# The transpose of the attention's probabilities, in one piece or in two halves of the keys

## The chip, the cores and the metric

The kernel runs on one core of a Trainium2 chip. The metric is the device time of one execution in microseconds (us); less is better. The times of the kernel before are 2897.93, 2901.62 and 2910.8 us, median 2901.62.

## What is computed

One encoder layer over 2048 tokens of width 1024. Cut to what matters here:

```python
h = rmsnorm(x)
c_q, c_kv, k_rope, dq, dk, dv = split(h @ w_in)
# head group A: 4 heads of latent attention, softmax over 2048 keys per query
s = einsum('bqhd,bkhd->bhqk', q_m, k_m) * scale
o_mla = einsum('bhqk,bkhd->bqhd', softmax(s), v_mla)
# head group B: 4 heads of differential attention, two softmax maps and a relative-position bias
s = einsum('bqhmd,bkhmd->bmhqk', dq, dk) * scale + bias
p = softmax(s);  a = p[:, 0] - lam * p[:, 1]
o_diff = rmsnorm(einsum('bhqk,bkhd->bqhd', a, dv)) * (1 - lam_init)
x = x + concat(o_mla, o_diff) @ w_out
x = x + square(relu(rmsnorm(x) @ w_up)) @ w_down
```

Everything is float32 at the inputs and outputs.

## The kernel before, in words

To keep float32's accuracy with 16-bit matmuls, most operands are split into a high and a low float16 part, and a product is made as high by high, high by low and low by high, summed in PSUM.

The program has four stages in order of time: the input projections (up to some 456 us), the attention (456 to about 1480 us), the output projection and the MLP's two products (a Strassen-like scheme of seven block products). The change touches the attention alone.

The attention runs over 4 heads and, in each, 16 blocks of 128 queries: 64 steps. A step makes, for one head and one query block, one softmax map of the MLA group (`soft[0]`, called d = 0) and two of the differential group (`soft[1]` and `soft[2]`, together d = 1). The work of a step, per map:

- **S** (line 735, TensorE): scores of 128 queries with 512 keys in one PSUM bank. Four chunks a map; five matmuls a chunk for MLA, two for the others: 36 in a step. There are seven PSUM banks for scores (tag D), so a chunk waits for an earlier one to be read.
- **M** (lines 745 and 750, VectorE): the maximum of each chunk, with the bias band added where it lies; **N** (755, 756): the shift of the exponential.
- **E** (line 762, ScalarE): the exponential into a float32 tile of 1024 keys (tag P; two a map, the halves hf = 0 and 1), with the row sum.
- **diff** (line 805, VectorE): for d = 1, the second map times a factor added to the first, a half at a time.
- **hi** (lines 812 and 140): the high float16 part of a half of the keys, by ScalarE for d = 1 and by GpSimd for d = 0; **lo** (line 819, GpSimd): the low part of a half, as the difference. Both go into the tile `hl[d]` (tag L).
- **T** (line 823): one DMA transpose for each d, issued by the queue of SyncE (SP): all 2048 keys, high and low part, 128 x 4096 float16, out of `hl[d]` into `pT[d]` (another L tile). There are seven L tiles.
- **pv** (lines 833 to 835, TensorE): the product with the values, in four parts of four key blocks (parts 0 and 1 use keys of the first half, 2 and 3 of the second), 12 matmuls a part, 96 in a step for both d. They add up in the one PSUM bank of tag O.
- **store** (839, ScalarE): the output scaled into an N2 tile (six of them), and a DMA to DRAM.

The order on each engine is written out by hand in the string `PROG`, run once a step: a token is an operation with its map and part. No mark means the current step, `'` the step before and `"` the one before that: T0' is the MLA transpose of the step before. `ordered` chains the instructions of each compute engine in this order. DMAs of this stage are not chained; they stand on SP's queue in the order that the planner gave them, and `set_fence` and `behind` keep certain loads (queries, keys, values, weights of the output projection) behind the last transpose issued before them. SP works off its queue in order: an issue that waits holds all behind it.

In PROG the operations of one step's d = 0 run: S, M, E in their own step, then `hi00 lo00 ... hi01 ... lo01` at its end, then in the next step `T0'` after S03 and `pv0'0` to `pv0'3`. Those of d = 1: `hi10'`, `hi11'` in the next step, `lo10" lo11" T1"` and `pv1"0` to `pv1"3` in the one after. So TensorE's order in a step is S00 to S03, S10 to S12, pv0'0, pv0'1, S13, pv0'2, S20, pv0'3, S21, S22, pv1"0, pv1"1, pv1"2, S23, pv1"3. GpSimd's is lo10", lo11", hi00, lo00, hi01, lo01.

Around the steps, `loads` fetches keys and values of the next head, one piece in a step, `load0` and `load1` fetch queries every fourth step, and in the last head `wo_step` prepares the weights of the output projection on VectorE and ScalarE. After the last step the program runs twice more with the first places empty, between parts of the output projection.

Of the kernel before, what the change touches and what calls it, by code (L numbers as in the profile page):

```python
# [13 lines left out]
F16 = mybir.dt.float16  # L14
BF16 = mybir.dt.bfloat16
AF = mybir.ActivationFunctionType
ALU = mybir.AluOpType
AX = mybir.AxisListType.X

P = 128  # L20
S = 2048
D = 1024
NT = S // P
# [27 lines left out]
def encoder_layer(ctx: ExitStack, tc: tile.TileContext, a, out, stop=None):  # L51
    nc = tc.nc
# [7 lines left out]
    def nm(s):  # L60
        uid[0] += 1
        return f"{s}_{uid[0]}"
# [3 lines left out]
    def sb(tag, shape, dt=F32):  # L66
        return work.tile(shape, dt, tag=tag, name=nm(tag), bufs=BUFS[tag])
# [16 lines left out]
    def pso():  # L84
        return psum.tile([P, 512], F32, tag="O", name=nm("O"), bufs=OB)
# [7 lines left out]
    def ordered(ins):  # L93

        e = ins.ins.engine
        if e in last:
            tc.add_manual_dep(ins.ins, last[e].name, NOSYNC, reason="order")
        last[e] = ins.ins
# [10 lines left out]
    def set_fence(*ins):  # L109
        for i in ins:  # L110
            fence[i.ins.engine] = i.ins
# [11 lines left out]
    G = nc.gpsimd  # L123
# [15 lines left out]
    def gscale(o, i, sc):  # L139
        return G.tensor_scalar(o, i, sc, 0.0, ALU.mult, ALU.add)  # L140
# [624 lines left out]
    class Step:  # L765
# [40 lines left out]

        def hi(self, d, hf):
            if hf == 0:
                self.hl[d] = sb("L", [P, 2, S], F16)
            o = self.hl[d][:, 0, 1024 * hf : 1024 * hf + 1024]  # L810
            if d:
                ordered(act(o, self.soft[d].p[hf], AF.Copy))  # L812
            else:
                ordered(gscale(o, self.soft[d].p[hf], 1.0))

        def lo(self, d, hf):
            c = slice(1024 * hf, 1024 * hf + 1024)
            hl = self.hl[d]
            ordered(G.tensor_tensor(hl[:, 1, c], self.soft[d].p[hf], hl[:, 0, c], ALU.subtract))  # L819

        def transpose(self, d):
            self.pT[d] = sb("L", [P, 2 * NT, P], F16)
            set_fence(nc.sync.dma_start_transpose(self.pT[d], self.hl[d].rearrange("p i k -> p (i k)")))

        def pv(self, d, part, parts):
            if part == 0:
                self.o[d] = pso()
            od = self.o[d][:, 0:P]
            n = NT // parts
            for kb in range(part * n, part * n + n):  # L830
                v = self.sl[d]["v"][kb // 8][:, kb % 8]
                hT_, lT_ = self.pT[d][:, kb, :], self.pT[d][:, NT + kb, :]
                ordered(mm(od, hT_, v[:, 0], start=kb == 0, stop=False))  # L833
                ordered(mm(od, hT_, v[:, 1], start=False, stop=False))  # L834
                ordered(mm(od, lT_, v[:, 0], start=False, stop=kb == NT - 1))  # L835
# [4 lines left out]
            dma(oD[self.qt][:, 4 * d + self.h, :], ob)  # L840

    PROG = """
    S00 M00 S01 S02 S03 load1 M01 T0' S10 M02 S11 lo10" M03 N0 E00 S12 pv0'0 E01 sums1' M10
    lo11" diff0' pv0'1 S13 pv0'2 S20 E02 M11 M12 E03 M13 pv0'3 N1 T1" S21 diff1' S22 M20 load0
    hi00 hi10' pv1"0 pv1"1 lo00 store0' hi01 M21 pv1"2 E10 E11 S23 E12 pv1"3 M22 M23 E13 N2 hi11' E20
    E21 lo01 E22 E23 rows1' sums0 store1"
    """

# [761 lines left out]
```

## Time and profile before

| | us |
|---|---|
| median of the three runs | 2901.62 |
| the profiled execution, its own time | 2907.15 |
| its span in the profile | 2905.4 |
| mean granted TensorE clock | 0.984 |
| attention, 45 full steps | 507.0 to 1190.0 |
| attention, 15 further steps in the last head | 1190.0 to 1421.35 |

The profile is of one execution. "Idle before" is time in which an engine had nothing to run before the instruction named, and behind the arrow stands what ended that time. Weight loads have an engine of their own in the profile (PEld) and run beside the matmuls (PE). DMA issues stand under SPq with the time that SP's sequencer spent on them; the landing is later.

### The profile page before, as it was taken

What the parts mean: (1) busy time and instruction counts of PE and PEld (TensorE: products, weight loads), DVE (VectorE), ACT (ScalarE), POOL (GpSimd) and SP (SyncE); (2) the same over time, 40 slices, a digit from 0 to 9 for tenths busy, and PEclk for the clock granted to TensorE, in tenths of its full rate; (3) what the DMA queues carried; (4) which work ended last, traced back from release to release, by engine and by line L of the source; (5) the groups of instructions that cost most, each with busy time, mean ns of one, the idle gap of its engine ahead of it and who ended that gap; (6) DMA issues with size and microseconds to landing.
All of it is one profiled execution on the core that took longest, in us unless ns stands there. A gap on an engine that the chain in (4) does not pass through costs nothing. (4 is left out here: it accounts for less than half of the span.)

```text
span 2905.4 us, 47553 instructions
## 1 busy us (share of the span) xinstructions
PE 2694.7 (93%) x16904; PEld 1576.4 (54%) x16904; DVE 2138.1 (74%) x4292; ACT 1742.2 (60%) x3814; POOL 1724.4 (59%) x1404
## 2 busy tenths in 40 slices
PE   7999998988899898889899989999999899999999
PEld 6878885655555565555555434444444344444444
DVE  8767778898888988899968777666666555555543
ACT  6544556887778888777847666666666433333332
POOL 5334435887778888778725366444444656555644
PEclk9999999999999999999999999999999999999999
DMA  5445566988888998889854654333334643333324
GB/s 191 121 118 128 138 143 166 200 196 180 182 190 185 198 193 195 196 192 195 204 178 145 227 157 145 131 131 130 130 123 162 235 160 124 113 130 131 131 94 175
DMA packets 990415, 469.31 MB, mean 162 GB/s; under 512 B 772032, under 2 KB 938944, under 8 KB 990176
## 3 DMA queue, kind: packets, MB, share of 16 engines
q1 hardware_dynamic: 990176, 466.27, 59.9%
q8 instruction: 132, 2.16, 0.3%
q14 instruction: 107, 0.88, 0.1%
HBM read 168.39 MB, written 132.12 MB: 103 GB/s over the span
## 5 line engine op out<-in xcount | busy, mean ns | idle before, releaser
L762 ACT ACTIVATE P<-D,nm,one 128x512 f32<-128x512 f32 x768 | 586.7, 775 | 149.4 <-DVE s L793 88.0
L735 PE MATMUL D<-W,X 128*128 128x512 f16 x2304 | 562.6, 383 | 23.6 <-ACT P L762 21.7
L819 POOL TENSOR_TENSOR L<-P,L 128x1024 f16<-128x1024 f32 x256 | 561.4, 2202 | 17.3 <-ACT L L812 6.5
L750 DVE TENSOR_REDUCE nmx<-D 128x1 f32<-128x512 f32 (+3 forms) x768 | 455.5, 621 | 65.6 <-PE D L735 59.1
L833 PE MATMUL O<-W,L 128*128 128x128 f16 x2048 | 368.5, 222 | 84.7 <-DMA L<-L 76.3
L1448 POOL TENSOR_TENSOR W<-W,N 128x512 f32<-128x512 f32 x192 | 242.7, 1274 | 227.9 <-DVE W L1446 222.7
L835 PE MATMUL O<-W,L 128*128 128x128 f16 x2048 | 368.1, 222 | 0.0
L834 PE MATMUL O<-W,L 128*128 128x128 f16 x2048 | 367.9, 222 | 0.0
L1446 DVE SCALAR_TENSOR_TENSOR W<-D,dsc,W 128x512 f32<-128x512 f32 x224 | 166.4, 747 | 263.1 <-PE D L136 263.1
L134 PE MATMUL D<-W,W 128*128 128x512 f16 (+2 forms) x822 | 314.2, 382 | 33.4 <-DVE P L1310 20.1
L735 PEld LDWEIGHTS <-X 128*128 128x128 f16 x2304 | 214.2, 99 | 231.8 <-issue 37.7
L140 POOL TENSOR_SCALAR L<-P 128x1024 f16<-128x1024 f32 x128 | 219.2, 1712 | 179.7 <-ACT P L762 179.7
L135 PE MATMUL D<-W,W 128*128 128x512 f16 (+2 forms) x822 | 313.6, 382 | 3.2 <-DVE W L130 3.2
L136 PE MATMUL D<-W,W 128*128 128x512 f16 (+2 forms) x822 | 313.4, 381 | 0.1
L833 PEld LDWEIGHTS <-L 128*128 128x128 f16 x2048 | 203.2, 99 | 151.7 <-DMA L<-L 123.4
L134 PE MATMUL D<-L,W 128*128 128x512 f16 (+1 forms) x644 | 249.5, 387 | 17.7 <-ACT X L1297 12.7
L134 PE MATMUL D<-L,P 128*128 128x512 f16 x648 | 247.8, 382 | 15.0 <-ACT N L1442 14.7
L135 PE MATMUL D<-L,P 128*128 128x512 f16 x648 | 247.5, 382 | 0.0
L136 PE MATMUL D<-L,P 128*128 128x512 f16 x648 | 247.5, 382 | 0.0
L136 PE MATMUL D<-L,W 128*128 128x512 f16 (+1 forms) x644 | 247.2, 384 | 0.0
L135 PE MATMUL D<-L,W 128*128 128x512 f16 (+1 forms) x644 | 247.1, 384 | 0.0
L834 PEld LDWEIGHTS <-L 128*128 128x128 f16 x2048 | 203.5, 99 | 31.0 <-issue 5.5
(421 smaller groups left out, 5731.5 us busy)
## 6 DMA issues: line engine op xcount, KB each, us to landing
P<-uD SPq DMA_DIRECT2D x124, 448.0 KB, 4.8
uD<-P SPq DMA_DIRECT2D x96, 512.0 KB, 3.2
P<-in_w_up_dram SPq DMA_DIRECT2D x34, 512.0 KB, 4.0
W<-in_w_down_dram SPq DMA_DIRECT2D x32, 512.0 KB, 4.4
X<-in_x_dram SPq DMA_DIRECT2D x17, 512.0 KB, 3.7
vD<-N SPq DMA_DIRECT2D x32, 256.0 KB, 2.6
qA<-N SPq DMA_DIRECT2D x32, 256.0 KB, 2.6
oD<-N SPq DMA_DIRECT2D x128, 64.0 KB, 2.4
```

Of the source, the lines that this page charges most:

```text
L134: mm(o, ah, bh, start=first, stop=False, skip_group_check=more),
L135: mm(o, ah, bl, start=False, stop=False, skip_group_check=more),
L136: mm(o, al, bh, start=False, stop=last, skip_group_check=more),
L140: return G.tensor_scalar(o, i, sc, 0.0, ALU.mult, ALU.add)
L735: ordered(mm(s, st, mv[:, kc], start=j == 0, stop=j == len(self.passes) - 1))
L750: ordered(V.tensor_reduce(self.nmx[:, self.n : self.n + 1], s[:, c0 * P : c1 * P], AX, ALU.max))
L762: last_exp[:] = [act(o, self.ch[c], AF.Exp, bias=self.nm, scale=self.sg, accum_out=self.sm[:, c : c + 1])]
L819: ordered(G.tensor_tensor(hl[:, 1, c], self.soft[d].p[hf], hl[:, 0, c], ALU.subtract))
L833: ordered(mm(od, hT_, v[:, 0], start=kb == 0, stop=False))
L834: ordered(mm(od, hT_, v[:, 1], start=False, stop=False))
L835: ordered(mm(od, lT_, v[:, 0], start=False, stop=kb == NT - 1))
L1448: G.tensor_tensor(x, x, part.pop((t, to)), ALU.add)
```

## The change

The transpose of each d becomes two, one for each half of the keys. The split tile `hl` is laid out with the half as the outermost index, so that the high and low part of a half lie together, and `pT` likewise. In `PROG` the second half's MLA transpose T01' takes the place of T0'; the first half's, T00, stands a step earlier, right behind lo00. Of the differential ones, T10" stands behind lo10" and T11" behind lo11"; T1" behind N1 goes. The products read their slices from the new places; they keep their places in the order.

```diff
         def hi(self, d, hf):
             if hf == 0:
-                self.hl[d] = sb("L", [P, 2, S], F16)
-            o = self.hl[d][:, 0, 1024 * hf : 1024 * hf + 1024]
+                self.hl[d] = sb("L", [P, 2, 2, 1024], F16)
+            o = self.hl[d][:, hf, 0]
...
         def lo(self, d, hf):
-            c = slice(1024 * hf, 1024 * hf + 1024)
-            hl = self.hl[d]
-            ordered(G.tensor_tensor(hl[:, 1, c], self.soft[d].p[hf], hl[:, 0, c], ALU.subtract))
-
-        def transpose(self, d):
-            self.pT[d] = sb("L", [P, 2 * NT, P], F16)
-            set_fence(nc.sync.dma_start_transpose(self.pT[d], self.hl[d].rearrange("p i k -> p (i k)")))
+            hl = self.hl[d][:, hf]
+            ordered(G.tensor_tensor(hl[:, 1], self.soft[d].p[hf], hl[:, 0], ALU.subtract))
+
+        def transpose(self, d, hf):
+            if hf == 0:
+                self.pT[d] = sb("L", [P, 2, NT, P], F16)
+            t = nc.sync.dma_start_transpose(self.pT[d][:, hf], self.hl[d][:, hf].rearrange("p i k -> p (i k)"))
+            set_fence(t)
...
-                hT_, lT_ = self.pT[d][:, kb, :], self.pT[d][:, NT + kb, :]
+                pT = self.pT[d][:, kb // 8]
+                hT_, lT_ = pT[:, kb % 8], pT[:, 8 + kb % 8]
...
     PROG = """
-    S00 M00 S01 S02 S03 load1 M01 T0' S10 M02 S11 lo10" M03 N0 E00 S12 pv0'0 E01 sums1' M10
-    lo11" diff0' pv0'1 S13 pv0'2 S20 E02 M11 M12 E03 M13 pv0'3 N1 T1" S21 diff1' S22 M20 load0
-    hi00 hi10' pv1"0 pv1"1 lo00 store0' hi01 M21 pv1"2 E10 E11 S23 E12 pv1"3 M22 M23 E13 N2 hi11' E20
+    S00 M00 S01 S02 S03 load1 M01 T01' S10 M02 S11 lo10" T10" M03 N0 E00 S12 pv0'0 E01 sums1' M10
+    lo11" T11" diff0' pv0'1 S13 pv0'2 S20 E02 M11 M12 E03 M13 pv0'3 N1 S21 diff1' S22 M20 load0
+    hi00 hi10' pv1"0 pv1"1 lo00 T00 store0' hi01 M21 pv1"2 E10 E11 S23 E12 pv1"3 M22 M23 E13 N2 hi11' E20
     E21 lo01 E22 E23 rows1' sums0 store1"
     """
```

## Rows read from the trace of the kernel before

**Rows 1.** The page's first part: busy us of each engine, its share of the whole span, and its instructions.
```profile
PE 2694.7 (93%) x16904; PEld 1576.4 (54%) x16904; DVE 2138.1 (74%) x4292; ACT 1742.2 (60%) x3814; POOL 1724.4 (59%) x1404
```

**Rows 2.** Busy time by stretch: two stretches of the attention, with the length, each engine's busy us and instructions, the granted TensorE clock, the share of the DMA engines and GB/s.
```profile
507.00:1190.00 683.00, 614.58 (x5938) 403.12 (x5937) 601.22 (x1388) 546.51 (x1274) 555.71 (x318) 0.98 0.88 191
1190.00:1421.35 231.35, 205.62 (x1984) 133.16 (x1982) 212.24 (x479) 181.86 (x426) 184.65 (x104) 0.99 0.86 194
```

**Rows 3.** The waits of TensorE between 507 and 1190 us: in total, times, longest.
```profile
PE O L833 <- DMA L<-L: 62.4, 51, 2.9
PE O L833 <- ACT P L762: 4.1, 3, 2.3
```

**Rows 4.** The same between 1190 and 1480 us.
```profile
PE O L833 <- DMA L<-L: 13.4, 11, 2.2
PE D L735 <- ACT P L762: 11.2, 22, 2.0
PE O L833 <- ACT N L839: 3.0, 4, 1.3
```

**Rows 5.** Of the page's costliest groups, the first product of a high part, over the whole span: busy us, mean ns, then the idle time before them and what ended it.
```profile
L833 PE MATMUL O<-W,L 128*128 128x128 f16 x2048 | 368.5, 222 | 84.7 <-DMA L<-L 76.3
```

**Rows 6.** TensorE in order of time, 907 to 936 us: start, duration, what, how many, and in brackets the idle time before it. Of runs of products only those at which the text stops are kept.
```profile
907.04 5.78 PE L735 MATMUL D<-W,X 128*128 128x512 f16 x26
912.65 0.22 PE L833 MATMUL O<-W,L 128*128 128x128 f16 x1
914.00 0.59 PE L735 MATMUL D<-W,X 128*128 128x512 f16 x2
...
917.13 0.22 PE L833 MATMUL O<-W,L 128*128 128x128 f16 x1
...
920.24 6.01 PE L735 MATMUL D<-W,X 128*128 128x512 f16 x26
927.88 0.23 PE L833 MATMUL O<-W,L 128*128 128x128 f16 x1 [1.63 <-DMA L<-L]
...
935.41 0.81 PE L735 MATMUL D<-W,X 128*128 128x512 f16 x3
```

**Rows 7.** ScalarE in the same steps: the first exponential of a step, the high part of d = 1, the store that frees the O bank, and the first exponential of the next step.
```profile
912.73 0.78 ACT L762 ACTIVATE P<-D,nm,one 128x512 f32<-128x512 f32 x1 [1.09 <-DVE nm L756]
...
915.76 1.06 ACT L812 ACTIVATE L<-P 128x1024 f16<-128x1024 f32 x1
916.71 0.37 ACT L839 ACTIVATE N<-O,r 128x128 f32<-128x128 f32 x1
...
925.92 0.78 ACT L762 ACTIVATE P<-D,nm,one 128x512 f32<-128x512 f32 x1
```

**Rows 8.** GpSimd in the same steps: hi00, lo00, hi01, lo01, a small product of row factors, then lo10" and lo11" together.
```profile
914.44 1.47 POOL L140 TENSOR_SCALAR L<-P 128x1024 f16<-128x1024 f32 x1 [4.62 <-ACT P L762]
916.00 2.13 POOL L819 TENSOR_TENSOR L<-P,L 128x1024 f16<-128x1024 f32 x1
918.09 2.02 POOL L140 TENSOR_SCALAR L<-P 128x1024 f16<-128x1024 f32 x1
920.19 2.13 POOL L819 TENSOR_TENSOR L<-P,L 128x1024 f16<-128x1024 f32 x1
922.28 0.19 POOL L801 TENSOR_TENSOR r<-r,vin 128x1 f32<-128x1 f32 x1
922.42 4.21 POOL L819 TENSOR_TENSOR L<-P,L 128x1024 f16<-128x1024 f32 x2
```

**Rows 9.** SP's queue in the same steps: start and time of issue. L823 is T, L116 a store or load, L588 a transposing load of keys or queries from DRAM.
```profile
914.62 0.54 SPq L116 DMA_DIRECT2D oD<-N  x1
915.21 1.27 SPq L588 DMA_TRANSPOSE W<-kR  x1
917.10 0.32 SPq L116 DMA_DIRECT2D oD<-N  x1
917.47 1.88 SPq L588 DMA_TRANSPOSE X<-qA  x1
922.35 3.99 SPq L823 DMA_TRANSPOSE L<-L  x1
...
926.66 4.06 SPq L823 DMA_TRANSPOSE L<-L  x1
```

**Rows 10.** Busy time by stretch, three neighbouring stretches of one step; the columns are those of rows 2.
```profile
895.00:899.30 4.30, 1.97 (x27) 1.48 (x26) 4.03 (x11) 3.86 (x9) 2.07 (x2) 0.97 1.30 258
899.30:902.40 3.10, 3.10 (x20) 2.00 (x18) 1.77 (x6) 0.23 (x1) 3.02 (x3) 0.50 0.64 150
902.40:907.04 4.64, 4.64 (x67) 3.93 (x66) 3.17 (x8) 3.77 (x10) 4.64 (x3) 0.99 0.21 51
```

**Rows 11.** The transposes of line 823 between 507 and 1190 us: time of issue on SP in ns as least/median/largest, the waits on SP before them, and the us from issue to landing.
```profile
L823 SPq DMA_TRANSPOSE L<-L x91: 3842/4062/5664, 508.1 to 1189.4; - x91
L823 SPq EVENT_SEMAPHORE  x90: 17/28/28, 512.0 to 1188.8; - x90
...
DMA to landing us min/median/max: 5.4/5.8/7.7
```

**Rows 12.** The same of line 588 over the whole span, for the transposing loads of queries, 512 x 512 float16 each.
```profile
L588 SPq DMA_TRANSPOSE X<-qA x16: 1325/2446/5119, 432.5 to 1339.7; - x16
L588 SPq DMA_TRANSPOSE X<-qB x16: 1332/2794/3892, 435.7 to 1369.9; - x16
```

**Rows 13.** VectorE in order of time: the last maximum of the MLA map in the step that began at 920.24.
```profile
924.75 0.69 DVE L750 TENSOR_REDUCE nmx<-D 128x1 f32<-128x512 f32 x1 [0.35 <-PE D L735]
```

## The prediction, made before the change was run

> **What bounds the kernel now.** I began with the busy shares of the whole span [rows 1]: TensorE 93%, no other engine above 74%, so at first sight a kernel of matmuls. The change sits in the attention alone, so I cut out that stage [rows 2]. The 683 us from 507 to 1190 us hold 5938 matmuls; a step has 36 for the scores and 96 for the products with the values, so these are 45 steps of 15.18 us. TensorE is busy 614.58 us (13.66 per step), VectorE 601.22 (13.36), GpSimd 555.71 (12.35), ScalarE 546.51 (12.14). Nobody is full: something makes them take turns. The waits of TensorE name it [rows 3]: 62.4 of its 68.4 idle us end with the landing of a transpose, before line 833, the first product of a group; another 13.4 us follow in the fourth head [rows 4]. The costliest groups of the page say the same over all 64 steps, 76.3 us [rows 5].
>
> What the wait is made of can be read from two steps [rows 6 to 9]. The scores of one step begin at 907.04, the next at 920.24 (13.20 later), the one after at 935.41 (15.17). From 907.04 to the first product at 912.65 are 26 matmuls, 0.216 us each, so the 20 of the MLA scores (S00 to S03) end at 911.36. Their maxima, then the exponentials from 912.73, then GpSimd in its own order: hi00 from 914.44, lo00 916.00 to 918.13, hi01 918.09, lo01 920.19 to 922.32. SP gives T0' out at 922.35, and TensorE resumes with pv0'0 at 927.88, after 1.63 us idle. That is 16.52 us from the end of S03; in TensorE's order pv0'0 stands only 912.65 - 911.36 = 1.29 us behind the next S03. A step can't be shorter than 16.52 - 1.29 = 15.23 us, and the mean is 15.18. **The chain scores, exponentials, split on GpSimd, transpose, product is the bound**, and no engine's sum is. In the short step before, T0' had been early enough.
>
> A stall has a second price: from 895.0 to 899.3 TensorE worked 1.97 of 4.30 us, and in the 3.1 us behind that the granted clock was 0.50, the 1.2 GHz level, then 0.99 [rows 10]; at half speed that loses 1.55 us. It lies in the 15.18 and is not counted again.
>
> **The change, part by part.** *The split tile in another order* (halves outermost) has the same elements, engines and contiguous runs of 1024: nothing. *The index of the products* only names other slices: nothing.
>
> *One transpose into two.* A whole one takes 4.06 us of issue on SP (median, 91 of them) and 5.8 us to landing [rows 11]. The one at 922.35 has 3.99 us of issue and 5.53 until TensorE resumes, so 1.54 us follow the issue [rows 6, 9]. No half from SBUF is in the trace. Bounds: issue in proportion to the bytes, 2.0 us, or no shorter, 4.06. The nearest rows are the transposes of 512 KB from DRAM, half of these: the one at 917.47 takes 1.88 us, and the least for the queries is 1.33, the median 2.45 [rows 9, 12]. I take 2.0 of issue and 2.0 + 1.54 = 3.54 to landing; the ends are 2.9 and 5.8. Four halves then hold SP 8.0 us a step, as two wholes did.
>
> By the Trainium skill, "DMA: Bandwidth & Descriptors", section on the anatomy of one DMA, a transfer costs a constant of about 2.0 us plus its bytes at 436 GB/s. That speaks against the change: by it, as an estimate, four halves cost 12.8 us where two wholes cost 8.8. The trace has 5.53 where this gives 4.4 for a whole, so I work with the row. Whether the constant is paid one after another is what decides, and there the trace stands against the rule: the whole issued at 922.35 lands about 927.88, and the next begins at 926.66 [rows 6, 9], before that landing. Only SP's own issue is serial.
>
> *Moved ahead.* The four halves need these: T00 lo00, T01' lo01, T10" lo10", T11" lo11". On the same two steps (the first GpSimd pair from 922.42 takes 4.21, so lo10" ends 924.5 and lo11" 926.63 [rows 8]), with 3.54 us to landing, measured from the end of S03 and less the place in TensorE's order at which each is wanted:
> T00: 921.7, wanted by pv0'0 at +1.29: step of at least 9.0.
> T01': 925.9, wanted by pv0'2 at +3.07 (914.00 and two matmuls): 11.4.
> T10": 928.1, wanted by pv1"0 at +5.77 (917.13): 10.9.
> T11": 930.2, wanted by pv1"2 at +7.12: 11.7.
> All are 1.5 us or more under the shortest steps seen. With landings 2.0 us longer (the upper bound) T11" asks for 13.7.
>
> *What is queued behind.* SP works in order and T00 waits for GpSimd, so what stands behind it waits too: store0' (917.10) and the load of queries (917.47) [rows 9] start up to 3 us later. The store frees one of six tiles and is read by the output projection, the queries are wanted steps later: nothing; without that cover a late load costs its 3 us every fourth step, 0.75 a step. Two more waits on SP a step cost 28 ns each [rows 11]. The pT tiles are taken earlier, by some 4 us for d=0 (after 918.1 instead of 922.35) and 2 us for d=1; four L tiles are handed out a step and there are seven. A split tile lives from 914.44 to 927.88, under a step, and so about 3.5 are alive at once: nothing. TensorE, GpSimd and ScalarE get no instruction more.
>
> **What is late next.** Two things stand close behind. One is the loop of ScalarE and TensorE: the four exponentials from 912.73, hi10' at 915.76, store0' at 916.71, which frees the one O bank for pv1"0 at 917.13, then the rest of the products, and the next S00 to S03 up to the next exponential at 925.92 [rows 6, 7]: 13.19 us, and between these two nothing waited for a transpose. The other is VectorE with 13.36 us of busy time a step; in the undisturbed pass it still waits 0.35 us for S03 [rows 13]. So a step after: 13.36 + 0.35 = 13.71. To this I add 0.25 for loads that run beside a half: the longest landing is 7.7 against 5.8 [rows 11], and 1.9 us in every eighth step is 0.24. Step: 13.96.
>
> **The sum.** 45 steps x (15.18 - 13.96) = 55 us. The stretch 1190 to 1421.35, fifteen steps of 15.42 with VectorE at 212.24 / 15 = 14.15 (it also works on the output weights there): 14.75 after, 15 x 0.67 = 10 us. The first steps and the hand-over to the output projection: 0 (0.5 us of transposes' waits there at the start). Total 65 us. The profiled execution took 2907.15 with a span of 2905.4, 0.2% above the median of 2901.62 (2897.93 to 2910.8); taken off the median: 2836.6, say 2837.
>
> **The rivals.** *A. The second halves stay late* (pv0'2 and pv1"2 take over half of the waits, because a half lands hardly sooner than a whole and loads come beside it). For: GpSimd still makes lo11" last, and landings go up to 7.7. Against: 1.5 us of room. A step of 14.6 gives 26 + 5 = 31 us: 2871. Chance 0.13.
> *B. Nothing changes.* The two halves of pT or of the split tile are handled as one, so that pv0'0 waits for the last writer of the whole tile, T01'; or the released wait goes to the exponentials and the O bank at once. For: ScalarE's store is already a releaser there, with 3.0 us in the fourth head [rows 4]. Against: clean steps of 13.2 exist. 2902. Chance 0.08.
> *C. Slower: SP's issue becomes the bound.* In the step shown SP had 0.54 + 1.27 + 0.32 + 1.88 = 4.0 us beside the transposes [rows 9]. Four halves fill a step of 15.18 from 2.8 us of issue each on; at 3.2 the step is 16.8 and the kernel 60 x 1.6 = 97 us slower, 2999; at 4.06 it is 20.2, 3200. Against: 1.88 for the same bytes from DRAM. For: a median of 2.45 to 2.79 there [rows 12], when traffic is heavy. Chance 0.06.
>
> **How the numbers follow.** The forecast has 0.73. Its own bounds: VectorE without any wait, 45 x 1.82 + 15 x 1.27 = 101 us, 2801; at the other end rival A. A range of 2803 to 2885 takes in A and leaves out B and C and the far ends, some 2 in 10. About 0.5%, 14.5 us, is what a measurement of this kernel can tell from no change: under 2887 are the forecast and A (0.86, less a little for an A that gives under 15 us), 0.08 are the same, and 0.07 slower (C, and smaller mishaps of its kind).
>
> **What would show it.** Right: 256 rows of line 823's successor with about 2.0 us of issue and 3.5 to 4 to landing; TensorE's wait for transposes in the 45 steps from 62.4 down to under 12 us; in its place waits at the products for ScalarE's store or an exponential; VectorE busy 95% or more of a step; steps of about 14 us; hardly a stretch at clock 0.5. Wrong: issue above 2.8 us per half (C); waits of the old size before pv0'2 and pv1"2 (A); pv0'0 starting with T01' (B); steps that stay above 14.8 us with VectorE and TensorE both idle.

## The result, and the profile after

The kernel after takes 2872.57 us (median of 4 runs, 2871.14 to 2876.13), beside 2905.2 us for the kernel before on the same chip: a ratio of 0.9891 with a 95% interval of 0.9864 to 0.9918. It is faster by 32.6 us where 65 were forecast: the direction is right and the time lies in the range, but half of the gain is missing. The profiled execution took 2871.79 us with a span of 2870.0, 35.4 less than the span before.

The first part of the page, as in [rows 1], shows the same work in less time:

```profile
PE 2687.7 (94%) x16904; PEld 1575.0 (55%) x16904; DVE 2130.1 (74%) x4292; ACT 1742.3 (61%) x3814; POOL 1721.8 (60%) x1404
```

Busy time by stretch in the kernel after; the stretches begin and end at the same steps as those of [rows 2] (45 steps, then 15):

```profile
505.97:1151.36 645.39, 604.56 (x5944) 398.34 (x5942) 594.83 (x1390) 544.33 (x1268) 555.10 (x317) 1.00 1.01 202
1151.36:1387.94 236.58, 208.56 (x1986) 135.76 (x1983) 211.33 (x479) 182.61 (x426) 184.19 (x105) 0.97 0.89 190
```

Cut at the first score of a step, the 45 steps took 683.79 us and now take 645.39: 38.4 less, 15.20 to 14.34 a step. The next 15 took 231.49 and now take 236.58: **5.1 more**. All the rest is 2.1 shorter. That is the whole of the 35.4. Of the 0.85 us a step in the first stretch, 0.61 are idle time of TensorE (1.52 to 0.91: the stretch less the busy time, by 45) and 0.23 are its own work (13.66 to 13.43 at a mean clock of 0.98, then 1.00). The second price of a stall, seen in [rows 10], did come back.

The waits of TensorE in the 45 steps, against [rows 3], and in the 15, against [rows 4]:

```profile
PE D L735 <- ACT P L762: 25.5, 35, 3.0
PE O L836 <- DMA L<-L: 10.3, 14, 1.8
PE D L735 <- DMA X<-qB: 3.8, 3, 1.8
```
```profile
PE D L735 <- ACT P L762: 23.4, 29, 5.2
PE O L836 <- ACT N L842: 3.4, 5, 0.9
```

The waits for transposes fell from 62.4 to 10.3 us, and from 13.4 to nothing. In their place stand scores (line 735) that wait for ScalarE's exponential to free their bank: 25.5 us in the 45 steps, where [rows 3] has a wait for the exponential only as 4.1 us and at another line, and 23.4 us in the last head, where [rows 4] has 11.2. The halves themselves (line 824 is now T), against [rows 11]:

```profile
L824 SPq DMA_TRANSPOSE L<-L x180: 1315/1710/4287, 508.1 to 1146.9; - x180
...
DMA to landing us min/median/max: 3.6/4.0/6.8
```

A half costs 1.71 us of issue and 4.0 to landing. So the transposes are cured, and something that ScalarE waits for is not. Here is its wait for a load in the 45 steps of the kernel after, then in the kernel before (507 to 1190 us):

```profile
ACT W L130 <- DMA P<-vD: 24.7, 11, 3.5
```
```profile
ACT W L130 <- DMA P<-vD: 2.7, 5, 0.8
```

Line 130 on ScalarE is the split of the next head's values into high and low parts, four times in the 16 steps of a head; it waits for a load from DRAM that SP gives out. (`load0` is the token at which the pieces of the next head, and in the last head those of the output weights, are given out; of the queries it is `load1` that goes out every fourth step.) One such step of the kernel after, first on SP's queue (answering [rows 9]; line 601 loads values, line 588 queries and keys), then on ScalarE, then on TensorE:

```profile
907.35 2.02 SPq L824 DMA_TRANSPOSE L<-L  x1
...
910.09 3.84 SPq L824 DMA_TRANSPOSE L<-L  x2
914.02 0.53 SPq L116 DMA_DIRECT2D oD<-N  x1
914.64 0.41 SPq L601 DMA_DIRECT2D P<-vD  x1
```
```profile
915.11 0.37 ACT L842 ACTIVATE N<-O,r 128x128 f32<-128x128 f32 x1
919.02 1.15 ACT L130 ACTIVATE W<-P,vsc 128x1024 f16<-128x1024 f32 x1 [3.54 <-DMA P<-vD]
920.07 0.76 ACT L762 ACTIVATE P<-D,nm,one 128x512 f32<-128x512 f32 x1
```
```profile
920.98 0.59 PE L735 MATMUL D<-W,X 128*128 128x512 f16 x2 [3.03 <-ACT P L762]
```

SP stands in T01', T10" and T11" until 913.9, the last two one right behind the other, so the values go out at 914.64 and are there at 919.0. ScalarE stands before them for 3.54 us with the exponentials of the second map behind it; the scores S23 want the bank that the first of these empties, and TensorE loses 3.03 us. All ten stalls of over 1 us for ScalarE in these 45 steps lie in a step with such a split or the one after it.

The loads themselves are not later than they were. Counted from the first score of the step in which it goes out, a load of values landed after 14.35 us before and after 14.12 us now (medians of eleven). What moved is ScalarE: it had done all that stands ahead of the split after 13.77 us before, and after 12.49 now. The split is not among the instructions that `ordered` chains, so the planner places it. In the kernel before it stood behind all four exponentials of the second map each time; in the kernel after it stands ahead of one, two or all four of them. Here is the same step in the kernel before, which began at 935.41 (after: 905.16), first SP, then ScalarE:

```profile
945.55 0.42 SPq L601 DMA_DIRECT2D P<-vD  x1
```
```profile
945.25 0.37 ACT L839 ACTIVATE N<-O,r 128x128 f32<-128x128 f32 x1
...
948.30 0.78 ACT L762 ACTIVATE P<-D,nm,one 128x512 f32<-128x512 f32 x1
...
949.76 1.15 ACT L130 ACTIVATE W<-P,vsc 128x1024 f16<-128x1024 f32 x1 [0.59 <-DMA P<-vD]
```

In the last head the loads are those of the output weights. VectorE between 1151 and 1388 us after, and between 1190 and 1421 before, waiting for them to take their maximum (line 900, before 897):

```profile
DVE rb_b L900 <- DMA W<-in_w_out_dram: 11.8, 5, 3.5
```
```profile
DVE rb_b L897 <- DMA W<-in_w_out_dram: 5.4, 4, 2.2
```

The worst of them in the kernel after, on SP, VectorE and ScalarE: four halves, with their waits, hold SP for 11.71 us, the weights go out at 1272.78, their maximum (line 900) stands ahead of the shift of the second map, and ScalarE has nothing to do for 6.75 us; TensorE's longest wait, 5.2 us, is this one.

```profile
1260.39 11.71 SPq L824 DMA_TRANSPOSE L<-L  x4
...
1272.78 0.43 SPq L884 DMA_DIRECT2D W<-in_w_out_dram  x1
```
```profile
1277.11 1.22 DVE L900 TENSOR_REDUCE rb_b<-W 128x1 f32<-128x1024 f32 x1 [3.51 <-DMA W<-in_w_out_dram]
```
```profile
1280.14 0.78 ACT L762 ACTIVATE P<-D,nm,one 128x512 f32<-128x512 f32 x1 [6.75 <-DVE nm L756]
```

Here too the load is not what moved. The eight blocks of weights that are searched for a maximum landed 13.96 us into their step before and 12.43 us now (medians), but VectorE was ready for them after 13.47 and now after 11.12: the planner, which places this maximum too, had put it behind the shift of the second map eight times, and now puts it ahead of it six times.

### The profile page after: what moved, and what is told of

Its sections match the earlier page's. It is cut to its first block, busy times and chain, and to the rows that moved or that the text cites. A ratio compares the mean times of both kernels' runs of the same rounds, so it can differ in the third digit from the quotient of the medians.

```text
span 2870.0 us, 47985 instructions
## 1 busy us (share of the span) xinstructions
PE 2687.7 (94%) x16904; PEld 1575.0 (55%) x16904; DVE 2130.1 (74%) x4292; ACT 1742.3 (61%) x3814; POOL 1721.8 (60%) x1404
## 5 line engine op out<-in xcount | busy, mean ns | idle before, releaser
L735 PE MATMUL D<-W,X 128*128 128x512 f16 x2304 | 570.7, 383 | 64.7 <-ACT P L762 58.8
L836 PE MATMUL O<-W,L 128*128 128x128 f16 x2048 | 361.1, 219 | 16.8 <-DMA L<-L 10.3
L837 PE MATMUL O<-W,L 128*128 128x128 f16 x2048 | 361.0, 219 | 0.6 <-DVE W L130 0.6
L838 PE MATMUL O<-W,L 128*128 128x128 f16 x2048 | 361.1, 219 | 0.0
L134 PE MATMUL D<-L,W 128*128 128x512 f16 (+1 forms) x644 | 249.3, 387 | 18.9 <-ACT X L1300 13.4
```

The costliest lines, as they stand in the source:

```text
L134: mm(o, ah, bh, start=first, stop=False, skip_group_check=more),
L735: ordered(mm(s, st, mv[:, kc], start=j == 0, stop=j == len(self.passes) - 1))
```

## The experiments

Two theories of the missing 32 us. **Late loads**: the halves make the room that was forecast, and loads that stand behind them on SP take half of it back. **The chain was read wrongly**, so that the room is smaller. A third, that the loads come when they came and the work that waits for them was placed too early, got no run of its own; runs 4, 5 and 7 bear on it. Ratios are against the kernel before on the same chip. "Step" is the mean of the 45 steps and, after a stroke, of the 15 (before 15.20 / 15.43, after 14.34 / 15.77); waits are TensorE's in the 45 steps. Lines have other numbers in some kernels: in runs 1 and 2 the first product is line 839; in runs 4, 5 and 7 to 10 line 741 is the scores, 756 a maximum, 768 the exponential, 842 the first product, 848 the store, 830 a half and 594 a load of queries; run 12 has 768 and 839.

**1 and 2. Each split alone.** T0' in halves and T1" whole; then the other way round:

```diff
 # 1, against the kernel after
-lo10" T10" ... lo11" T11" ... pv0'3 N1 S21
+lo10" ... lo11" ... pv0'3 N1 T1" S21
 # 2, against the kernel after
-S03 load1 M01 T01' ... lo00 T00
+S03 load1 M01 T0' ... lo00
```

> Only the MLA transpose is in two halves (T00, T01'); the differential one stays whole, behind N1. Theory 'one chain, two ends': the whole T1" still asks for a step of 926.63 + 5.53 - 911.36 - 5.77 = 15.0 us where T0' asked for 15.2, so nearly nothing is won: 2893 to 2902 us, and TensorE's waits for transposes move to pv1"0. Rival 'each stall counts for itself': the waits before pv0'0, some three fifths of all, go, and with them three fifths of the gain of 33 us: about 2885.

Measured: 2907.9 us, ratio 1.0005 (0.9995 to 1.0015), step 15.12 / 15.62. No gain, as expected of one of two chains that bind alike, though 6 us above the range that was given.

> Only the differential transpose is in two halves (T10", T11"); the MLA one stays whole. Theory 'one chain, two ends': T0' still asks for 15.2 us a step, so no gain: 2900 to 2908 us, all waits for transposes before pv0'0. Rival 'each stall counts for itself': two fifths of 33 us are won: about 2892.

Measured: 2888.83 us, ratio 0.9935 (0.9923 to 0.9946), step 14.77 / 15.60: a miss of the theory by 11 us, near the rival. The waits of TensorE, first of run 1, then of run 2:

```profile
PE O L839 <- DMA L<-L: 43.8, 30, 4.1
PE D L735 <- DMA X<-qB: 12.6, 9, 2.5
```
```profile
PE O L839 <- DMA L<-L: 45.7, 40, 3.6
```

Either whole transpose that is left still holds TensorE for some 45 us, so both chains have to be cut. Run 1 has late loads too: TensorE waits 12.6 us for queries, and ScalarE 14.5 us for values, where in run 2 it waits 1.8. In both the split stands behind all four exponentials, as in the kernel before; in run 1 the values land after 15.51 us of the step, in run 2 after 14.45. Why run 2 gains 19 us and run 1 none is told by this only in part, and stays open.

**3. The halves at the old places**, T00' T01' where T0' stood and T10" T11" where T1" stood:

```diff
-S03 load1 M01 T01' ... lo10" T10" ... lo11" T11" ... N1 S21 ... lo00 T00
+S03 load1 M01 T00' T01' ... lo10" ... lo11" ... N1 T10" T11" S21 ... lo00
```

> Both transposes in halves, but each pair of halves given out where the whole one was (T00' T01' behind S03 of the next step, T10" T11" behind N1). With the measured 1.7 us of issue and 4.0 to landing of a half the chain asks for 13.65 (T00'), 13.6 (T01'), 13.5 (T10") and 13.9 us (T11") a step, all under the 14.34 that the changed kernel has. Theory 'the shorter landing is enough': 2872 to 2882 us. Rival 'the early start of the first half is what counts': at least half of the gain is lost, 2889 or more.

Measured: 2903.88 us, ratio 0.9985 (0.9976 to 0.9993), step 14.86 / 15.73. By the numbers the early places seem to be the gain. The trace says otherwise; TensorE between 506 and 1175 us, then ScalarE:

```profile
PE D L735 <- ACT P L762: 33.5, 31, 4.8
PE O L836 <- DMA L<-L: 8.8, 12, 2.3
```
```profile
ACT W L130 <- DMA P<-vD: 41.3, 11, 5.2
```

The transposes are as little waited for as in the kernel after, and ScalarE waits 41.3 us for values instead of 24.7. Again they land when they did (14.42 us into the step), but the planner has put the split ahead of all four exponentials, all eleven times. The 45 steps:

```profile
509.32:1178.22 668.90, 622.64 (x5943) 407.50 (x5941) 597.72 (x1393) 544.20 (x1271) 556.07 (x318) 0.97 0.96 195
```

Of the 23.5 us that these steps are longer than in the kernel after, only 5.4 are idle time of TensorE; 18.1 are its own work, at a mean clock of 0.97. That the longer stalls (up to 4.8 us) brought the clock down is likely after [rows 10], and no run shows it apart. Run 10 tells whether the places of the halves matter.

**4, 5 and 6. The loads, one kind at a time**, each in the kernel after: the values loaded a step ahead and their split tied to the place of `load0` in PROG; the maximum of the output weights tied to the place of `load0`, with no load moved; the second load of queries moved a step ahead.

```diff
 # 4
             if qt in VQ:
-                split_v(i // 2, h, kv[i // 2, h], raw_v(i // 2, h, i % 2, "P"))
+                split_v(i // 2, h, kv[i // 2, h], raws.pop())
+            if qt + 1 in VQ:
+                i = VQ.index(qt + 1)
+                raws.append(raw_v(i // 2, h, i % 2, "L"))
 # 5 (4 does the same with the split): tied to the last ordered instruction of the engine
-        behind(V.tensor_reduce(wmx[:, k : k + 1], raw, ...))
+        pinned(V.tensor_reduce(wmx[:, k : k + 1], raw, ...))
 # 6
-                qs = qnext.pop(), load_q(1, h, qt // 4)
+                qs = qnext.pop(0), qnext.pop(0)
...
+            if qt % 4 == 3 and n + 1 < NT * H:
+                fetch[0] = lambda f=fetch[0]: (f(), qnext.append(load_q(1, ...)))
```

> The changed kernel, with each load of values for the next head issued a step earlier (into an L tile), and its split held at the place of the token load0. Theory 'loads behind the halves on SP are late for those who want them': ScalarE's 24.7 us of waits for values in the 45 steps go, and with them the waits of S23, S01 and S03 behind such a split: 15 to 25 us less than the changed kernel, 2848 to 2858. Rival 'VectorE is the floor, waits only move': under 5 us less, 2868 to 2873.

Measured: 2867.85 us, ratio 0.9863 (0.985 to 0.9876), step 14.24 / 15.56: a miss, at the time of the rival. ScalarE's wait is gone as expected, the gain is not: most of it came back as waits for transposes, 22.8 us between 506 and 1150 us instead of 10.3:

```profile
PE O L842 <- DMA L<-L: 22.8, 19, 4.1
PE D L741 <- ACT P L768: 2.9, 15, 0.4
```

This run moves the load and places the split at once, so it doesn't tell which of the two ends ScalarE's wait.

> The changed kernel, with VectorE's maximum of each block of the output weights held at its own step's token load0, a step behind its load, where the planner had put it 4 us behind the load. Theory 'loads behind the halves are late': VectorE's 11.8 us of waits for these weights in the fourth head go, and the fourth head's S23 waits with them: 8 to 12 us less than the changed kernel, 2860 to 2865. Rival 'VectorE is the floor': 2870 to 2873.

Measured: 2867.33 us, ratio 0.9862 (0.9846 to 0.9878), step 14.52 / 14.79. The last head falls from 15.77 to 14.79, where the forecast had 14.75, and no load was moved for it: the place of the maximum on VectorE alone is worth some 15 us here. The 45 steps, which this edit doesn't touch by intent, came out 0.17 longer, with 30.3 us of ScalarE's waits for values instead of 24.7; so the time ends 2 us above what was expected.

> The changed kernel, with the differential queries of the next four steps fetched behind the last score of the fourth step, at its token load0, and not at the start of the step that uses them. Theory 'loads behind the halves are late': the 3.8 us of waits of S10 for queries go, and the query load no longer stands between T00 and T01' on SP: 3 to 8 us less than the changed kernel, 2864 to 2870. Rival 'waits only move': 2871 to 2875.

Measured: 2876.09 us, ratio 0.9893 (0.9879 to 0.9907), step 14.32 / 15.81: nothing by itself, near the rival.

**7. All three together.**

> The changed kernel with all three: values a step ahead, the maxima of the output weights a step behind their load, queries ahead. Theory 'loads behind the halves are late': what the forecast had and the change did not give comes back, 26 to 40 us less than the changed kernel: 2832 to 2847, a step of 13.8 to 14.0 us in the first three heads. Rival 'VectorE is the floor, waits only move': 2860 or more.

Measured: 2858.01 us, ratio 0.9832 (0.9819 to 0.9846), step 14.27 / 14.79: a miss by 11 us. The largest wait that is left is at pv0'2 for T01': 16.3 of 30.9 us, and only in steps whose number leaves 2 when divided by four. One of these on SP, then the first product that waited:

```profile
776.89 2.99 SPq L830 DMA_TRANSPOSE L<-L  x1
779.93 2.28 SPq L594 DMA_TRANSPOSE X<-qA  x1
782.30 1.67 SPq L830 DMA_TRANSPOSE L<-L  x1
```
```profile
L842 PE MATMUL O<-W,L x2: 289/302/314, 788.2 to 788.5; 128*128 128x128 f16 x2
...
  DMA L<-L: 3.6, 1
```

GpSimd had ended lo01 at 778.9, but T01' goes out at 782.30: SP first gave out T00, late, and then the first load of queries, load1, which stands right ahead of T01' in PROG.

**8. The same loads with whole transposes**, as a control:

> The kernel before, whole transposes and all, with the same three changes of loads. Theory 'the loads became late through the change': the chain over the whole transposes still sets the step, 15.2 us, and the loads cost little there (2.7 us of waits for values, 5.4 for output weights): 2895 to 2905 us. Rival 'the loads are a cost of their own, whatever the transposes': 26 us or more less than before, 2879 or less.

Measured: 2917.36 us, ratio 1.0037 (1.0022 to 1.0051), step 15.43 / 15.31: 12 us above what was expected. Without the halves, moving the loads gains nothing and costs a little.

**9. Run 7 with load1 behind T11".**

```diff
-    S00 M00 S01 S02 S03 load1 M01 T01' S10 M02 ...
-    lo11" T11" diff0' pv0'1 ...
+    S00 M00 S01 S02 S03 M01 T01' S10 M02 ...
+    lo11" T11" load1 diff0' pv0'1 ...
```

> All loads out of the way as in the kernel at 2858.0, and also the load of queries of load1 issued behind T11" instead of right ahead of T01'. In that kernel 16.3 us of TensorE's waits in steps 3 to 47 stood at pv0'2 for the landing of T01', all in steps of which the number leaves 2 when divided by four, which is where this load goes out. Theory that T01' is late because the load stands ahead of it on SP's queue: pv0'2's waits under 5 us, step 14.27 to 13.95 or so, time 2840 to 2848. Rival that the transfer itself, not the place, delays the halves (or that T10" or T00 are now late in its stead): pv1"2, pv1"0 or pv0'0 wait 10 us or more, time 2853 to 2860.

Measured: 2840.24 us, ratio 0.9777 (0.9754 to 0.9799): 64 us faster than before, as forecast for the change itself, and the fastest version. Step 13.92 / 14.80, where the forecast had 13.96 / 14.75. Its two stretches, then the waits of TensorE and of VectorE in the first:

```profile
506.64:1133.16 626.52, 605.07 (x5944) 397.88 (x5941) 589.55 (x1391) 544.09 (x1272) 559.05 (x316) 1.00 1.04 208
1133.16:1355.10 221.94, 203.66 (x1986) 133.26 (x1984) 210.77 (x478) 180.57 (x421) 184.95 (x106) 1.00 0.98 204
```
```profile
PE O L842 <- DMA L<-L: 9.3, 17, 1.0
PE O L842 <- ACT N L848: 6.2, 8, 1.0
PE D L741 <- ACT P L768: 4.3, 23, 0.4
```
```profile
DVE nmx L756 <- PE D L741: 17.7, 56, 0.4
```

No wait of TensorE is longer than 1.0 us there. It is busy 605.07 of 626.52 us (97%) and VectorE 589.55 (94%), with 17.7 more before a score, 0.39 a step, where [rows 13] had 0.35.

**10. The halves at the old places again, with the loads of run 7.**

> Halves at the old places (T00' T01' where T0' stood, T10" T11" where T1" stood), with the loads of values, output weights and queries out of the way. Theory that the early start of the first halves is worth little by itself and that the halves at the old places lost their gain to late value loads (S23 waited 33 us for ScalarE in steps 3 to 47): that wait under 8 us, step from 14.86 to 14.1 to 14.3, time 2853 to 2868. Rival that the early start is the gain: step 14.7 or more, transposes' waits at pv0'0 and pv1"0 over 20 us, time 2880 or more.

Measured: 2853.99 us, ratio 0.982 (0.9797 to 0.9844), step 14.18 / 15.01; ScalarE's share of TensorE's waits fell from 33.5 to 4.2 us:

```profile
PE O L842 <- DMA L<-L: 22.7, 23, 2.2
PE D L741 <- ACT P L768: 4.2, 23, 0.4
```

So the early places are worth nothing beside run 7; beside run 9, with load1 out of the way, this was not tried. The traces show why: a half goes out when its own low part is there, wherever it stands in PROG, as long as nothing that waits longer stands ahead of it on SP. Over 43 steps the median from the end of the low part to the issue of T00 is 0.03 us in the kernel after and in run 3 alike (the mean 0.27 and 1.23), that of T10" under 0.1 in both. The places decide only what the loads and stores stand behind.

**11. A longer chain**: in the kernel before, lo01 made twice.

```diff
-    E21 lo01 E22 E23
+    E21 lo01 lo01 E22 E23
```

> The kernel before, with the last low part of the MLA map (lo01) made twice in a row on GpSimd: 2.13 us more ahead of T0' and, as GpSimd goes on at once with lo10" and lo11", ahead of T1" too; nothing else. GpSimd's sum rises from 12.35 to 14.5 us a step, still under the step. Theory that the chain from a step's scores over the transpose to the scores that follow spans two steps: half of it a step, 1.07 us, 60 to 64 steps, 64 to 75 us, time 2965 to 2980. Rival, the reading of the prediction that the chain spans one step: 2.13 us a step, 128 to 136 us, time 3033 or more. Under 2940: neither chain binds.

Measured: 2986.52 us, ratio 1.0276 (1.0248 to 1.0303): 82 us more. Between 505.58 and 1251.29 us, the 45 steps, and TensorE's waits there:

```profile
505.58:1251.29 745.71, 636.89 (x5943) 420.25 (x5941) 633.85 (x1389) 548.77 (x1273) 659.17 (x362) 0.95 0.81 175
```
```profile
PE O L833 <- DMA L<-L: 102.2, 56, 4.3
```

A step is 1.38 us longer, not 2.13. From the end of S03 to the product pv0'0 that needs it the mean rose by 2.02 us (17.40 to 19.42), so the 2.13 did enter the chain; but that way and the one from this product to the S03 behind it span two steps. The second rose by 0.69 us (12.96 to 13.65), and half of the two rises together is 1.36 of the 1.38. TensorE's own work is 14.15 us a step instead of 13.66 at the clock of 0.95, which would account for most of the second rise, and so for the 7 us above the upper end of what was expected; no run shows that apart.

**12. All loads as in run 9, with whole transposes.**

> The kernel before with whole transposes and every load where the kernel at 2840.2 has it (values, output weights and queries moved, load1 behind T1"). Theory that the halves make the room and the places of the loads only keep it: whole transposes still hold the chain over two steps, waits for transposes at pv0'0 and pv1"0 over 40 us in steps 3 to 47, step 15.0 or more, time 2893 to 2918. Rival that the places of the loads are the gain by themselves: time 2870 or less.

Measured: 2904.36 us, ratio 0.9995 (0.9986 to 1.0004), step 15.04 / 15.38. Its 45 steps, and what TensorE waits for:

```profile
507.26:1184.19 676.93, 606.28 (x5944) 397.00 (x5942) 593.67 (x1392) 545.38 (x1272) 557.78 (x319) 0.99 0.90 193
```
```profile
PE O L839 <- DMA L<-L: 58.4, 46, 3.1
```

The places of the loads give nothing without the halves, and the halves give half without the places. So the missing 32 us are the price of loads and of the work that waits for them, and of where both stand: runs 9 and 12 show it for all of them together. By the steps, 15 of the 32 lie in the last head, where run 5 shows that the place of the maximum on VectorE is enough. In the 45 steps run 9 against run 7 shows the price of load1 ahead of T01', some 17 us of the whole time. What the place of the value loads and the place of their split cost one without the other is not shown; the landings in the result speak for the split.

## Why the prediction was right in direction and wrong in size

**What bounds the kernel: right in what, wrong in how many steps.** The transposes did hold TensorE, and with the halves the waits before the products fell to 10.3 us, under the 12 that were given. But "a step can't be shorter than 16.52 - 1.29 = 15.23 us" is wrong. In TensorE's order pv0'0 of the next step stands behind that step's S03, and ahead of the S03 of the step after. The loop is S03, pv0'0, S03 with two steps in it. On [rows 6] it has 16.52 us to pv0'0 at 927.88 and 11.85 to the end of the S03 behind it (935.41, and 4.32 for the MLA scores): 28.37 for two steps, 13.20 and 15.17, or 14.19 each. As a mean over 43 steps the two links are 17.40 and 12.96, half of which is the 15.18; that these sums fit is no proof, since both are counted from S03 to S03. But the step of 13.20, which the prediction itself names, is shorter than its bound, and run 11 fits two steps better than one, with 1.38 us a step for 2.13 in the chain. That one link less 1.29 gave 15.23, so near the mean, was chance. It didn't spoil the sum, which rested on what comes next.

**One transpose into two: sizes near.** Issue 1.71 us (2.0 taken), landing 4.0 (3.54 taken). The "DMA: Bandwidth & Descriptors" page of the Trainium skill (anatomy of one DMA) has a constant of about 2.0 us, in a fit for transfers issued from GpSimd, where these are issued by SP. The trace comes near that constant: 5.8 for a whole and 4.0 for a half make 1.8 us for 512 KB and a constant of 2.2. But it isn't paid one after another, as was argued: four halves take 6.8 us of issue a step (4 x 1.71) where two wholes took 8.1.

**Moved ahead: right for three of the four, and the places were not needed.** T01' was not early enough in the steps in which load1 goes out ahead of it: 16.3 us of waits in run 7, 2.2 in run 9. The list of what each half needs names its low part and no load on SP. For the places, runs 3 and 10.

**What is queued behind: the step that failed.** "The store frees one of six tiles ... the queries are wanted steps later: nothing." That names the two rows of one step and leaves out the loads that stand there in other steps: of values, of output weights, and of queries ahead of T01'. The cover was named for the queries alone. The term was put at nothing and measured 32 us, the way from 2872.57 to 2840.24. Not all of it is the wait on SP that the sentence speaks of: the 15 us of the last head went in run 5 without a load being moved. And before, ScalarE waited 2.7 us for values in all, because it came to them late itself; now it waits 24.7, for loads that land no later in the step, because its split stands ahead of exponentials that it stood behind. That work which PROG doesn't chain would keep its place was taken for granted. The price that was given for a late load without cover, "3 us every fourth step, 0.75 a step", is about what the runs show: 3.03 us in the step above, 25.5 us or 0.57 a step in all, 18.6 of them in the ten long stalls. The row of line 130 was there to be read, in the waits of ScalarE.

**What is late next: right in size, when it could act.** 13.96 a step was forecast, 14.34 measured, and 13.92 with the loads out of the way; 14.75 in the last head, 15.77 measured and 14.80. In run 9 TensorE and VectorE fill the step together (13.45 and 13.10 busy, 0.39 waited), much as in "13.36 + 0.35 + 0.25", with less work in VectorE and more gaps. In part that is luck. TensorE's own 13.66 us stood above VectorE's 13.36 and was in neither the sum nor its bound of 2801; in run 9 it is TensorE that is nearer to full, and no run tells which of the two sets the step. And the 0.25 was for loads beside a half: of the halves in the kernel after with no instruction packet in flight (see the last section), the 68 with a load beside them landed in 4.01 us (median) and the 55 without in 3.78. The forecast gave 55 + 10 = 65 us; the kernel after gives 38 - 5, run 9 57 + 10 against the same steps.

**The rivals.** A had the right time (2871) for the wrong reason: the second halves take nearly all that is left of the waits for transposes, but that is 9.5 of TensorE's 39.6 us of waits in the 45 steps. B and C are out: 62.4 to 10.3 us, and 1.71 of issue; of B's second half, that the released wait goes to the exponentials at once, there is a part, the 25.5 us. Nobody in the list was late because of a load, which should have been the first of them.

## What to carry to other kernels

When an issue that waits is moved ahead on an in-order queue, list everything that ever stands behind it, over a whole period of the program and not one step, with who waits for it and how late it already is; a load that is just in time before is late once its reader comes sooner. Look at the reader as much as at the load: work that the program doesn't chain may stand elsewhere in the new kernel. A load that must not be late goes out a step early, and none stands between a producer and the transfer on which the next stage waits. A bound read from a loop needs the number of steps that the loop spans: follow it back to the same instruction, and test it by making one link longer.

## What the runs showed of the hardware

A transfer's landing varied together with traffic that no line of the kernel issues. The queues in run 7 between 783 and 787 us: share of the DMA engines and GB/s in 40 slices of 0.1 us, and the packets, MB and share of the queue that carries instructions:

```profile
DMA  9999999999999005000000000000000009999999
GB/s 292 292 292 287 294 274 259 269 266 269 223 136 8 0 0 164 0 0 0 0 0 0 0 0 0 8 8 10 8 10 10 10 13 236 287 292 287 289 289 289
...
q8 instruction: 1, 0.02, 1.5%
```

Around one packet of 16 KB of instructions the DMA engines moved next to nothing for 2 us, in the middle of a half that then took 5.85 us to land (782.30 to 788.15). In the kernel after, of the 180 halves in the 45 steps the 57 with such a packet between issue and landing took 5.20 us (median), the other 123 took 3.86; of the 91 whole transposes before, 31 took 7.14 and 60 took 5.64. No run varied these packets, so that they are the cause is only argued.
